# S5 phase tables: from GpSimd beside layer 0's first projections to VectorE beside layer 0's FFN

## The chip, the cores and the metric

One core of one Trainium2 chip runs the whole program. The metric is the device time of one execution in microseconds (us), and lower is better. The engines are called as the profile calls them: PE is TensorE's matmul, PEld its weight load, DVE is VectorE, ACT is ScalarE, POOL is GpSimd, and SP is SyncE, which here only issues DMAs (SPq is its queue).

## What is computed

The reference is a backbone block of two layers over 512 latent tokens and 256 context tokens of width 1024. Layer 0 mixes with SSD heads and RG-LRU blocks, layer 1 with HGRN2 heads and S5 groups, and a convolutional FFN of width 2816 stands behind each mixer. What the change touches is the S5 scan of layer 1, a complex diagonal recurrence with 16 groups of 64 states in each of two directions:

```
step = exp(log_step);  mag = exp(lam_re * step)
ar, ai = mag * cos(lam_im * step), mag * sin(lam_im * step)
h[t] = (ar + i ai) * h[t-1] + x[t]          (all 768 tokens, context first)
y = Re(h) c_re - Im(h) c_im
```

The kernel runs this recurrence over blocks of 8 tokens, 96 blocks in all. It turns the values of block n by the angle n times theta, where theta is 8 times lam_im times step, scans with the real factor mag to the power 8, and turns back. The cosines and sines of n times theta for n = 0 to 95, one row for each of 128 states (two directions of 64) and each of 16 groups, are the **phase tables** Ec and Es. They depend on parameters alone, not on the tokens.

## The kernel before

Everything is float32, and each big product is split into three matmuls of rounded halves (a high and a low part of both operands). The streams of the engines are put in order when the program is built: the build places instructions by their order in the source and by modelled times, so that neighbouring generators interleave on an engine, and each engine then runs its stream strictly in that order.

- **First projections of layer 0** (`xbc_phase`, L698). Twelve blocks of 128 channels, two to a weight panel of 256 columns. Each block takes 24 matmuls of 512 columns and 24 of 256, a four-tap convolution by ACT and DVE (L644) that reads the results from PSUM, SiLU, and a transpose. Beside them run the time-step path (`dt_phase`, L755), the modulation ticks and `s5_tables` (L827). The loop at L1200 calls one step of `s5_tables` for about 0.9 steps of `xbc_phase`.
- **`s5_tables`**. Step by step: lambda and step size are loaded, ar and ai are made, the reciprocal of the norm, then m8 (mag to the power 8) and, by three doublings of the angle (`twice`, L901), cosine and sine of theta. Then the phase tables (L919 to L933): starting from column 0 they are doubled seven times, from n columns to 2n, each time by one complex product (`cmul`, L892, six instructions: four multiplications, one subtraction, one addition). The constant ECV is 0, so all of them run on GpSimd over 16 groups at once; six more angle doublings run on DVE (18 instructions of 16 elements in a row). GpSimd's own DMA queue writes both tables to DRAM (`e_d`). The steps after that, on DVE, take powers of ar and ai (KP, eight copies at L952 to L955), load B and C, and multiply them (L974, `products` L988, `matrices` L1008).
- **Rest of layer 0's mixer**: the SSD steps, the RG-LRU, and the output projection. SSD is where GpSimd has its next work.
- **Layer 0's FFN** (`ffn`, L1383). Channel blocks f in groups of 8, 8 and 6. For each f there are gate and up projections, a 3 by 3 convolution on DVE, SiLU, and a product; for each group of f there are 8 output blocks m. Behind each f, each m of the first two groups, and the first four m of the last, `next(fill)` takes one step of a generator given from outside. At L1605 that generator is `l1_consts()` (one step) followed by 38 modulation ticks. A tick of `MT[3] = 5` makes five parts of the modulation vector: a 128 KB piece of `w_mod` comes by a DMA that SP issues, and DVE multiplies and adds it into `macc` (two instructions of 256 elements).
- **Layer 1**. The S5 scan (`quarter`, L1648) reads `e_d` back, four groups at a time (L1668), while layer 1's projections run.

The lines of the table before are these:

```
while n < 96:
    w = min(n, 96 - n)
    cmul(Ec[:, :, n:n + w], Es[:, :, n:n + w], Ec[:, :, 0:w], Es[:, :, 0:w],
         bc_mid(uc, w), bc_mid(us, w), et[:, :, :w], G if n > ECV else V)
    n *= 2
    if n < 96:
        uc, us = twice(f"v{n}", uc, us)
G.dma_start(e_d[0], Ec)
G.dma_start(e_d[1], Es)
```

Of the kernel before, what the change touches and what calls it, by code (L numbers as in the profile page):

```python
# [1 line left out]

# [1 line left out]

# [5 lines left out]
F32 = mybir.dt.float32  # L10
F32R = mybir.dt.float32r
AF = mybir.ActivationFunctionType
ALU = mybir.AluOpType
# [4 lines left out]
T = 768  # L18
# [10 lines left out]
MT = (1, 1, 4.5, 5, 1, 6, 1)  # L29
# [7 lines left out]
PSG = 0  # L37
# [11 lines left out]
ECV = 0  # L49
# [10 lines left out]
def bc_mid(ap, n):  # L60

    return ap.unsqueeze(2).broadcast_to([ap.shape[0], ap.shape[1], n])


def build(tc, I, out, dbg=None):
    nc = tc.nc
    V, S, G, PE, SP = nc.vector, nc.scalar, nc.gpsimd, nc.tensor, nc.sync
    if dbg is not None and "wrap" in dbg:
        V, S, G, PE, SP = [dbg["wrap"](e, n) for e, n in ((V, "V"), (S, "S"), (G, "G"), (PE, "PE"), (SP, "SP"))]
    es = ExitStack()  # L70
    cp = es.enter_context(tc.tile_pool(name="const", bufs=1, reuse_waits="tile"))
# [10 lines left out]
    def stt(o, a, s, b, op0, op1, eng=None):  # L82
        return (eng or V).scalar_tensor_tensor(o, a, s, b, op0=op0, op1=op1)  # L83


    def psx(name="px"):
        return pp.tile([128, 512], F32, tag="px", name=name, bufs=3)

    def psc(name="pc", n=256):
        return pp.tile([128, n], F32, tag="pc", name=name, bufs=2)  # L90
# [4 lines left out]
    def dump(name, ap):  # L95
        if dbg is not None and name in dbg:
            SP.dma_start(dbg[name], ap)
# [9 lines left out]
    def hcols(a, b):  # L107
        return [(HH[:, k, a:b], HL[:, k, a:b]) for k in range(8)]
# [129 lines left out]
    def mod_advance(q):  # L238

        q["stages"].pop(0)()  # L240
        if not q["stages"]:
            PEND.remove(q)
# [82 lines left out]
    def mod_tick():  # L325


        i = TICK[0]
        if i == NQ * LIM[0]:
            return  # L330
        l, j = MODSEQ[i // NQ]
        n = 1 if l == 1 and j >= 8 else 2
        if i % NQ == 0:
            MACC.append(macc())
        TICK[0] += 1
        mod_load()
        acc = MACC[-1]
        for k in range(8 // NQ):
            for e in range(n):
                prev = zero.broadcast_to([128, 256]) if i % NQ == 0 and k == 0 else acc[:, e]  # L340
                stt(acc[:, e], MST[i][:, k, :], sc[:, i % NQ * (8 // NQ) + k, e:e + 1], prev, ALU.mult, ALU.add)
        if i % NQ == NQ - 1:

            mod_pend(l, j, n, acc, LAG)
# [161 lines left out]
    def chain(*gs_):  # L506
        for g in gs_:
            yield from g
# [47 lines left out]
    for c, s_ in enumerate(src):  # L556
        t = ldp.tile([128, D], F32, tag=f"xin{c}", name=f"xin{c}")
# [55 lines left out]
    def mtick(r):  # L613
        for q in list(PEND):
            mod_advance(q)
        TA[0] += r
        while TA[0] >= 1.0:
            TA[0] -= 1.0
            mod_tick()
# [13 lines left out]
    h = hcols(0, T)  # L633
# [189 lines left out]
    kp_d = dr.tile([16, 16, 240], F32, name="kp_d")  # L823
    e_d = dr.tile([2, 128, 16, 96], F32, name="e_d")
    m8 = cp.tile([128, 16], F32, name="m8")

    def s5_tables():  # L827
        with tc.tile_pool(name="s5t", bufs=1, reuse_waits="tile") as tp:
            def t16(nm, shape=None):
                return tp.tile(shape or [128, 16], F32, name=nm, tag=nm)  # L830
# [58 lines left out]
            V.tensor_sub(zi, zi, ta)  # L889
            V.tensor_mul(zi, zi, den)  # L890

            def cmul(or_, oi, ar_, ai_, br, bi, t, eng):  # L892

                eng.tensor_mul(or_, ar_, br)
                eng.tensor_mul(t, ai_, bi)
                eng.tensor_sub(or_, or_, t)
                eng.tensor_mul(oi, ar_, bi)
                eng.tensor_mul(t, ai_, br)
                eng.tensor_add(oi, oi, t)

            def twice(nm, uc, us):  # L901

                c2, s2 = t16(f"{nm}c"), t16(f"{nm}s")
                stt(s2, uc, 2.0, us, ALU.mult, ALU.mult)
                stt(c2, us, -2.0, us, ALU.mult, ALU.mult)
                V.tensor_scalar(c2, c2, 1.0, None, op0=ALU.add)
                return c2, s2

            yield

            V.tensor_mul(m8, mag, mag)
# [1 line left out]
            V.tensor_mul(m8, m8, m8)  # L913
            uc, us = cs_, sn
            for i in range(3):
                uc, us = twice(f"u{i}", uc, us)
            yield

            with tc.tile_pool(name="s5e", bufs=1, reuse_waits="tile") as ep:  # L919
                Ec, Es = ep.tile([128, 16, 96], F32, name="Ec"), ep.tile([128, 16, 96], F32, name="Es")  # L920
                et = ep.tile([128, 16, 64], F32, name="et")
                V.memset(Ec[:, :, 0:1], 1.0)
                V.memset(Es[:, :, 0:1], 0.0)
                n = 1
                while n < 96:
                    w = min(n, 96 - n)
                    cmul(Ec[:, :, n:n + w], Es[:, :, n:n + w], Ec[:, :, 0:w], Es[:, :, 0:w],
                         bc_mid(uc, w), bc_mid(us, w), et[:, :, :w], G if n > ECV else V)
                    n *= 2
                    if n < 96:  # L930
                        uc, us = twice(f"v{n}", uc, us)
                G.dma_start(e_d[0], Ec)
                G.dma_start(e_d[1], Es)  # L933
            yield

            KP = [t16("kpr", [128, 9, 16]), t16("kpi", [128, 9, 16])]
            V.memset(KP[0][:, 0, :], 1.0)
# [4 lines left out]
            for k in (1, 2, 4):  # L942

                top = [KP[q][:, k:k + 1, :].broadcast_to([128, k, 16]) for q in range(2)]
                cmul(KP[0][:, k + 1:2 * k + 1, :], KP[1][:, k + 1:2 * k + 1, :], KP[0][:, 1:k + 1, :], KP[1][:, 1:k + 1, :],
                     top[0], top[1], kt[:, :k, :], V)
# [25 lines left out]
            bb = [t16("bbr", [128, 16, 16]), t16("bbi", [128, 16, 16])]  # L972
            tq = t16("tq", [128, 16, 16])
            cmul(bb[0], bb[1], B[0], B[1], bc_mid(zr, 16), bc_mid(zi, 16), tq, V)  # L974

            bs = [t16("bsr", [128, 16, 48]), t16("bsi", [128, 16, 48])]
# [220 lines left out]
    with tc.tile_pool(name="xbc", bufs=2, side="right", reuse_waits="tile") as xp:  # L1197
        s5t = s5_tables()
        acc = 0.0
        for i, _ in enumerate(xbc_phase(xp)):  # L1200
            acc += S5T
            while acc >= 1.0:
                acc -= 1.0
                next(s5t, None)
            if i == SSD0:
                for _ in s5t:
                    pass
                ssdp = sp_ctx.enter_context(tc.tile_pool(name="ssd", bufs=2, reuse_waits="tile"))
                ssd = ssd_phase(ssdp)
            if i >= SSD0 and (i - SSD0) % 2 == 0:  # L1210
                next(ssd)
# [290 lines left out]
    X = [xfp.tile([128, T], F32, name=f"xf{k}") for k in range(8)]  # L1502
# [14 lines left out]
    wfirst = [[], []]  # L1517
# [6 lines left out]
    norm = Norm(stats, X, T, lambda tag, n: ssdp.tile([128, n], F32, tag="xw" if tag == "diag" else "xt", name=tag, bufs=2), h, 0, "gffn", 3)  # L1524
    rest = norm.early()
# [19 lines left out]
    def lower_bound(pool):  # L1545
        l0, l1 = PS("lbl", 0, 6), PS("lbl", 6, 6)
        t = [pool.tile([128, 6], F32, name=f"lbt{i}") for i in range(7)]
        mx, e0, e1, s_, x_, a, b = t
        V.tensor_tensor(mx, l0, l1, op=ALU.max)
        for src, e in ((l0, e0), (l1, e1)):  # L1550
            V.tensor_sub(x_, src, mx)
            act(e, x_, AF.Exp)
            V.tensor_scalar(e, e, 1e-37, None, op0=ALU.max)
            act(a, e, AF.Ln)
            V.tensor_sub(a, x_, a)
            V.tensor_scalar(a, a, 1.0, 0.0, op0=ALU.add, op1=ALU.max)
            V.tensor_mul(e, e, a)
        V.tensor_add(s_, e0, e1)
        V.reciprocal(s_, s_)
        V.tensor_mul(e0, e0, s_)  # L1560
        V.tensor_mul(e1, e1, s_)
        V.tensor_add(e1, e0, e1)
        V.tensor_sub(lb, e1, e0)
        V.tensor_scalar(omlb, lb, -1.0, 1.0, op0=ALU.mult, op1=ALU.add)

    def l1_consts():
        with tc.tile_pool(name="l1c", bufs=1, reuse_waits="tile") as cp1:
            lower_bound(cp1)
        yield
# [17 lines left out]
    def nxt0(stats, pool):  # L1587
# [9 lines left out]
        def fin(pools):  # L1597
            for k in range(8):
                SP.dma_start(x2_d[k], X[k][:, XS])
                dump(f"x2_{k}", X[k])  # L1600
            FP.extend([norm, rest, pools])
        return rest, mid, fin

    FP = []
    ffn(0, X, T, norm, rest, wfirst, done0, h, nxt0, chain(l1_consts(), (mtick(MT[3]) for j in range(38 + 4 * PSG))))  # L1605
    norm, rest, pools = FP
    blk = [(psx(), psc()) for d in range(2)]

# [359 lines left out]
    X = []  # L1968
# [74 lines left out]
    h = hcols(0, 512)  # L2043
    norm = Norm(stats, X, 512, lambda tag, n: xqp.tile([128, n], F32, tag=tag, name=tag, bufs=2), h, 1, "gffn", 3)
    rest = norm.early()
# [67 lines left out]
```

## Time and profile before

| what | value |
|---|---|
| median of 3 runs | 2139.82 us (2135.62 to 2142.2) |
| the profiled execution | 2138.01 us, its span in the trace 2136.3 us |
| PE, PEld | 2022.4 us (95%), 1699.5 us (80%) |
| DVE | 1571.1 us (74%) |
| ACT | 872.8 us (41%) |
| POOL | 273.0 us (13%) |
| mean granted TensorE clock | 0.975 |

The span runs from the first to the last instruction of the trace, and 1.7 us of the profiled execution lie around it. Busy shares are means over stages with different limits, so the stage in which a piece of work lies has to be looked at by itself. In a timeline each line is one instruction or a run of equal ones: start, duration, engine, source line, operation, output and inputs, and in brackets the idle time before it with what ended that idle time. Two DVE instructions can overlap a little at their ends, so the distance from one start to the next is what an instruction costs in a busy stream, and its duration is slightly more.

### The profile page before, as it was taken

How to read it: one execution, taken by the hardware profiler on the slowest of the kernel's cores; microseconds unless marked ns; L12 is line 12 of the kernel's file. 1: busy time of each engine (PE TensorE's matmuls, PEld its weight loads, DVE VectorE, ACT ScalarE, POOL GpSimd, SP SyncE). 2: the span in 40 equal slices, each digit the busy share in tenths (PEclk: the TensorE clock that was granted, in tenths of full speed). 3: DMA queues.
4: the chain of work that ended last, by engine and by line, in shares of the span. 5: the costliest groups of instructions: out<-in, count | busy, mean ns of one | idle time of the engine just before them, and what ended most of it. 6: DMA issues, size and time to landing. Idle time of an engine off the chain costs nothing.

```text
span 2136.3 us, 32686 instructions
## 1 busy us (share of the span) xinstructions
PE 2022.4 (95%) x12738; PEld 1699.5 (80%) x12738; DVE 1571.1 (74%) x2916; ACT 872.8 (41%) x1276; POOL 273.0 (13%) x234
## 2 busy tenths in 40 slices
PE   8969989898898999999999999999999899999998
PEld 4848778787677888888888888897877688888887
DVE  5898898767778888868765656656876678667484
ACT  4625577586533442212321323324444344223234
POOL 2142333344421000000000000110011100000000
PEclk9979899999999999999999999999999999999999
DMA  9437535435676322333234112554421123222321
GB/s 332 132 102 206 152 98 168 123 97 165 225 242 215 99 87 94 112 121 116 94 118 139 62 50 94 152 160 147 126 71 58 40 80 99 97 82 98 99 84 55
DMA packets 283019, 261.09 MB, mean 122 GB/s; under 512 B 23406, under 2 KB 263061, under 8 KB 282865
## 3 DMA queue, kind: packets, MB, share of 16 engines
q1 hardware_dynamic: 257504, 243.35, 35.8%
q10 hardware_dynamic: 24464, 13.75, 2.3%
q8 instruction: 100, 1.64, 0.3%
q0 software_dynamic: 896, 1.90, 0.2%
q14 instruction: 55, 0.44, 0.1%
HBM read 224.17 MB, written 34.78 MB: 121 GB/s over the span
## 4 chain that ended last, share of the span: by engine, by line
PE 62%; DVE 6%; DMA 4%; POOL 1%; issue 1%; ACT 1%; SPq 0%; POOLq 0%; DVEq 0%; ACTq 0%
PE px L215 34%; PE pc L215 10%; PE pu L215 6%; PE pseg L215 4%; DMA mst<-in_w_mod_dram 1%; DVE macc L83 1%; PE pmodt L352 1%; PE pv L222 1%; PE pv L223 1%; PE pv L224 1%; POOL kc L1816 1%; PE plv L1858 1%; PE pob L215 1%; DMA xt<-xtok_d 0%; PE py L1711 0%
## 5 line engine op out<-in xcount | busy, mean ns | idle before, releaser
L80 ACT ACTIVATE whi<-st 128x1024 fp32r<-128x1024 f32 (+1 forms) x197 | 203.4, 1037 | 565.3 <-PE pc L215 365.1
L215 PE MATMUL px<-HH,whi 128*128 128x512 f32 (+2 forms) x1016 | 407.8, 403 | 15.3 <-DVE xbct L83 7.9
L215 PE MATMUL px<-HH,wlo 128*128 128x512 f32 (+2 forms) x1016 | 404.4, 398 | 0.0
L215 PE MATMUL px<-HL,whi 128*128 128x512 f32 (+2 forms) x1016 | 403.4, 397 | 0.9 <-DVE HL L83 0.9
L193 DVE TENSOR_TENSOR wlo<-st,whi 128x1024 fp32r<-128x1024 f32 (+1 forms) x197 | 237.5, 1209 | 78.3 <-ACT whi L80 76.3
L83 DVE SCALAR_TENSOR_TENSOR macc<-mst,sc,macc 128x256 f32<-128x256 f32 x434 | 216.9, 530 | 65.9 <-DMA mst<-in_w_mod_dram 64.8
L83 DVE SCALAR_TENSOR_TENSOR fa<-px,par,fa 128x441 f32<-128x441 f32 (+2 forms) x352 | 241.8, 691 | 8.2 <-ACT fa L80 2.2
L215 PEld LDWEIGHTS px<-HH,whi 128*128 128x128 f32 (+1 forms) x1016 | 192.0, 189 | 59.5 <-issue 9.6
L215 PEld LDWEIGHTS px<-HL,whi 128*128 128x128 f32 (+1 forms) x1016 | 191.8, 189 | 44.5 <-DVE HL L83 1.9
L215 PEld LDWEIGHTS px<-HH,wlo 128*128 128x128 f32 (+1 forms) x1016 | 191.8, 189 | 43.7
L215 PE MATMUL pc<-HH,whi 128*128 128x256 f32 x728 | 207.2, 286 | 4.6 <-ACT ge L80 3.2
L215 PE MATMUL pc<-HH,wlo 128*128 128x256 f32 x728 | 206.9, 285 | 0.0
L215 PE MATMUL pc<-HL,whi 128*128 128x256 f32 x728 | 206.9, 285 | 0.0
L215 PEld LDWEIGHTS pc<-HH,whi 128*128 128x128 f32 x728 | 137.8, 190 | 8.0 <-ACT ge L80 4.0
L80 ACT ACT_TABLE_LOAD x104 | 133.4, 1283 | 19.2 <-issue 5.4
L215 PEld LDWEIGHTS pc<-HL,whi 128*128 128x128 f32 x728 | 138.2, 190 | 1.1
L215 PEld LDWEIGHTS pc<-HH,wlo 128*128 128x128 f32 x728 | 138.2, 190 | 0.5
L215 PE MATMUL px<-fhi,wlo 128*128 128x512 f32 x304 | 120.4, 396 | 0.0
L215 PE MATMUL px<-fhi,whi 128*128 128x512 f32 x304 | 120.3, 396 | 0.0
L215 PE MATMUL px<-flo,whi 128*128 128x512 f32 x304 | 119.8, 394 | 0.0
L1815 POOL TENSOR_TENSOR kc<-kc,e 128x255 f32<-128x255 f32 x6 | 7.1, 1181 | 853.0 <-ACT kc L80 675.6
L215 PE MATMUL pu<-HH,wlo 128*128 128x512 f32 (+1 forms) x192 | 74.3, 387 | 0.0
(645 smaller groups left out, 4291.1 us busy)
## 6 DMA issues: line engine op xcount, KB each, us to landing
mst<-in_w_mod_dram SPq DMA_DIRECT2D x312, 128.0 KB, 2.2
st<-in_ffn_w_gate_dram SPq DMA_DIRECT2D x22, 1024.0 KB, 5.0
st<-in_ffn_w_up_dram SPq DMA_DIRECT2D x22, 1024.0 KB, 5.0
st<-in_ev_w_in_dram SPq DMA_DIRECT2D x18, 1024.0 KB, 6.4
st<-in_ffn_w_down_dram SPq DMA_DIRECT2D x16, 1024.0 KB, 5.0
bc<-cum_d SPq DMA_DIRECT2D x24, 512.0 KB, 6.2
sth<-in_od_w_in_dram SPq DMA_DIRECT2D x24, 512.0 KB, 4.0
st<-in_w_mod_dram SPq DMA_DIRECT2D x9, 1024.0 KB, 11.6
```

Of the source, the lines that this page charges most:

```text
L80: return S.activation(o, i, f, bias=bias, scale=scale, **kw)
L83: return (eng or V).scalar_tensor_tensor(o, a, s, b, op0=op0, op1=op1)
L193: (eng or V).tensor_sub(lo, src, hi.bitcast(F32))
L215: PE.matmul(o, ww[:, k, :M], hh[k][part][:, sl], start=(first and q == 0 and a == 0), stop=(stop and q == last and a == 2))
L222: PE.matmul(o, hh[k][0][:, sl], whi[:, k % 4, :], start=(k == 0), stop=False)
L223: PE.matmul(o, hh[k][0][:, sl], wlo[:, k % 4, :], start=False, stop=False)
L224: PE.matmul(o, hh[k][1][:, sl], whi[:, k % 4, :], start=False, stop=(k == 7))
L352: PE.matmul(pt[:, 2 * h_ + e:2 * h_ + e + 1], acc[:, e, h_ * 128:(h_ + 1) * 128], ones[:, 0:1], start=True, stop=True)
L1815: G.tensor_mul(kc[:, 0, 0:255], kc[:, 0, 0:255], e0[:, 0:255])
L1816: G.tensor_mul(kc[:, 1, 1:256], kc[:, 1, 1:256], e1[:, 1:256])
L1858: PE.matmul(v3[r:r + 32, c, :], kk(j), qq(j), start=True, stop=True, tile_position=(0, r))
```

## The change

The functions `cmul` and `twice` move out of `s5_tables`. `s5_tables` now only keeps cosine and sine of theta in a small constant tile `u8`, and has one step fewer. A new generator `s5_phases` makes the six doubled angles, and then builds the tables for four groups at a time on DVE, with the same doublings, in four steps for each four groups; SP issues the two writes to `e_d` for each. A new helper `both_of` advances two generators together. The FFN of layer 0 now gets `l1_consts()` followed by `s5_phases()` on one side and the 38 modulation ticks on the other, one step of each for each `next(fill)`.

```diff
@@ -1,4 +1,5 @@
 from contextlib import ExitStack
+from itertools import zip_longest
 
 import numpy as np
 
@@ -823,6 +824,48 @@
     kp_d = dr.tile([16, 16, 240], F32, name="kp_d")
     e_d = dr.tile([2, 128, 16, 96], F32, name="e_d")
     m8 = cp.tile([128, 16], F32, name="m8")
+    u8 = cp.tile([128, 2, 16], F32, name="u8")
+
+    def cmul(or_, oi, ar_, ai_, br, bi, t, eng):
+
+        eng.tensor_mul(or_, ar_, br)
+        eng.tensor_mul(t, ai_, bi)
+        eng.tensor_sub(or_, or_, t)
+        eng.tensor_mul(oi, ar_, bi)
+        eng.tensor_mul(t, ai_, br)
+        eng.tensor_add(oi, oi, t)
+
+    def twice(pool, nm, uc, us):
+
+        c2, s2 = [pool.tile([128, 16], F32, name=nm + x, tag=nm + x) for x in "cs"]
+        stt(s2, uc, 2.0, us, ALU.mult, ALU.mult)
+        stt(c2, us, -2.0, us, ALU.mult, ALU.mult)
+        V.tensor_scalar(c2, c2, 1.0, None, op0=ALU.add)
+        return c2, s2
+
+    def s5_phases():
+
+        with tc.tile_pool(name="s5e", bufs=1, reuse_waits="tile") as ep:
+            lad = [(u8[:, 0], u8[:, 1])]
+            for i in range(6):
+                lad.append(twice(ep, f"v{i}", *lad[-1]))
+            yield
+            for g in range(0, 16, 4):
+                gs_ = slice(g, g + 4)
+                Ec, Es = [ep.tile([128, 4, 96], F32, name=x, tag=x) for x in ("Ec", "Es")]
+                et = ep.tile([128, 4, 64], F32, name="et", tag="et")
+                V.memset(Ec[:, :, 0:1], 1.0)
+                V.memset(Es[:, :, 0:1], 0.0)
+                for i, (uc, us) in enumerate(lad):
+                    n = 1 << i
+                    w = min(n, 96 - n)
+                    cmul(Ec[:, :, n:n + w], Es[:, :, n:n + w], Ec[:, :, 0:w], Es[:, :, 0:w],
+                         bc_mid(uc[:, gs_], w), bc_mid(us[:, gs_], w), et[:, :, :w], V)
+                    if i in (3, 4, 5):
+                        yield
+                SP.dma_start(e_d[0, :, gs_], Ec)
+                SP.dma_start(e_d[1, :, gs_], Es)
+                yield
 
     def s5_tables():
         with tc.tile_pool(name="s5t", bufs=1, reuse_waits="tile") as tp:
@@ -889,23 +932,6 @@
             V.tensor_sub(zi, zi, ta)
             V.tensor_mul(zi, zi, den)
 
-            def cmul(or_, oi, ar_, ai_, br, bi, t, eng):
-
-                eng.tensor_mul(or_, ar_, br)
-                eng.tensor_mul(t, ai_, bi)
-                eng.tensor_sub(or_, or_, t)
-                eng.tensor_mul(oi, ar_, bi)
-                eng.tensor_mul(t, ai_, br)
-                eng.tensor_add(oi, oi, t)
-
-            def twice(nm, uc, us):
-
-                c2, s2 = t16(f"{nm}c"), t16(f"{nm}s")
-                stt(s2, uc, 2.0, us, ALU.mult, ALU.mult)
-                stt(c2, us, -2.0, us, ALU.mult, ALU.mult)
-                V.tensor_scalar(c2, c2, 1.0, None, op0=ALU.add)
-                return c2, s2
-
             yield
 
             V.tensor_mul(m8, mag, mag)
@@ -913,25 +939,10 @@
             V.tensor_mul(m8, m8, m8)
             uc, us = cs_, sn
             for i in range(3):
-                uc, us = twice(f"u{i}", uc, us)
-            yield
-
-            with tc.tile_pool(name="s5e", bufs=1, reuse_waits="tile") as ep:
-                Ec, Es = ep.tile([128, 16, 96], F32, name="Ec"), ep.tile([128, 16, 96], F32, name="Es")
-                et = ep.tile([128, 16, 64], F32, name="et")
-                V.memset(Ec[:, :, 0:1], 1.0)
-                V.memset(Es[:, :, 0:1], 0.0)
-                n = 1
-                while n < 96:
-                    w = min(n, 96 - n)
-                    cmul(Ec[:, :, n:n + w], Es[:, :, n:n + w], Ec[:, :, 0:w], Es[:, :, 0:w],
-                         bc_mid(uc, w), bc_mid(us, w), et[:, :, :w], G if n > ECV else V)
-                    n *= 2
-                    if n < 96:
-                        uc, us = twice(f"v{n}", uc, us)
-                G.dma_start(e_d[0], Ec)
-                G.dma_start(e_d[1], Es)
-            yield
+                uc, us = twice(tp, f"u{i}", uc, us)
+            yield
+            for q, t_ in enumerate((uc, us)):
+                V.tensor_copy(u8[:, q], t_)
 
             KP = [t16("kpr", [128, 9, 16]), t16("kpi", [128, 9, 16])]
             V.memset(KP[0][:, 0, :], 1.0)
@@ -1601,8 +1612,13 @@
             FP.extend([norm, rest, pools])
         return rest, mid, fin
 
+    def both_of(*gs_):
+
+        for _ in zip_longest(*gs_):
+            yield
+
     FP = []
-    ffn(0, X, T, norm, rest, wfirst, done0, h, nxt0, chain(l1_consts(), (mtick(MT[3]) for j in range(38 + 4 * PSG))))
+    ffn(0, X, T, norm, rest, wfirst, done0, h, nxt0, both_of(chain(l1_consts(), s5_phases()), (mtick(MT[3]) for j in range(38 + 4 * PSG))))
     norm, rest, pools = FP
     blk = [(psx(), psc()) for d in range(2)]
 
```

## Rows read from the trace of the kernel before

**Rows 1.** windows of four stretches: length, then busy PE, PEld, DVE, ACT, POOL, PEclk, DMA, GB/s

```profile
98.00:129.20 31.20, 19.67 (x100) 16.10 (x98) 30.96 (x86) 13.43 (x19) 26.39 (x44) 0.87 0.16 55
129.20:150.00 20.80, 11.65 (x75) 7.51 (x76) 20.80 (x36) 1.93 (x3) 0.09 (x1) 0.66 0.42 117
150.00:200.00 50.00, 50.00 (x329) 42.69 (x330) 44.36 (x74) 20.44 (x34) 4.99 (x5) 0.98 0.68 195
785.00:900.00 115.00, 115.00 (x674) 100.96 (x673) 94.86 (x175) 32.63 (x40) 0.00 (x0) 1.00 0.34 110
```

**Rows 2.** PE's timeline, 110 to 155 us: the three longest waits

```profile
119.58 0.45 PE L970 MATMUL ps5c<-ident,cst 128*128 128x128 f32 x1 [5.62 <-DVE xbct L83]
...
132.18 0.76 PE L215 MATMUL px<-HH,whi 128*128 128x512 f32 x1 [7.88 <-DVE xbct L83]
...
147.12 0.42 PE L1018 MATMUL pkp<-n,bsr 128*48 128x128 f32 x2 [3.06 <-DVE kp L1023]
```

**Rows 3.** POOL's timeline, 80 to 420 us: first and last of the tables, and the next

```profile
98.09 0.29 POOL L895 TENSOR_TENSOR et<-Es,u2s 128x16 f32<-128x16 f32 x1 [35.30 <-DVE u2c L83]
...
128.71 0.58 POOL L933 DMA_DIRECT2D e_d<-Es  x1 [0.30 <-POOL Es L899]
194.68 1.09 POOL L1109 TENSOR_SCALAR_AFFINE_SELECT bc<-bc 128x1024 f32<-128x1024 f32 x1 [65.40 <-DMA bc<-cum_d]
```

**Rows 4.** DVE's timeline, 80 to 205 us: instructions beside POOL's, and alone

```profile
108.87 0.72 DVE L952 COPY pwr<-kpr 64x144 f32<-64x144 f32 x1
...
110.67 0.60 DVE L954 COPY pqr<-kpr 64x128 f32<-64x128 f32 x1
...
115.66 1.10 DVE L803 TENSOR_TENSOR wend<-wend,dtv 128x192 f32<-128x192 f32 x1
116.68 0.74 DVE L83 SCALAR_TENSOR_TENSOR xbct<-px,par,xbct 128x511 f32<-128x511 f32 x1
...
121.33 1.30 DVE L895 TENSOR_TENSOR tq<-bi,zi 128x256 f32<-128x256 f32 x1
...
126.33 0.41 DVE L898 TENSOR_TENSOR tq<-bi,zr 128x256 f32<-128x256 f32 x1
126.67 0.28 DVE L979 COPY bsr<-bbr 64x256 f32<-64x256 f32 x1
...
127.31 1.25 DVE L980 COPY bsr<-bbr 64x256 f32<-64x256 f32 x1
...
128.87 0.29 DVE L980 COPY bsi<-bbi 64x256 f32<-64x256 f32 x1
129.19 0.75 DVE L83 SCALAR_TENSOR_TENSOR xbct<-px,par,xbct 128x511 f32<-128x511 f32 x1
```

**Rows 5.** the same timeline: small instructions and the starts of the next

```profile
105.32 0.16 DVE L83 SCALAR_TENSOR_TENSOR v64c<-v32s 128x16 f32<-128x16 f32 x1
105.41 0.32 DVE L894 TENSOR_TENSOR kpr<-kpr 128x32 f32<-128x32 f32 x1
...
107.71 0.21 DVE L895 TENSOR_TENSOR kt<-kpi 128x64 f32<-128x64 f32 x1
107.85 0.21 DVE L897 TENSOR_TENSOR kpi<-kpr,kpi 128x64 f32<-128x64 f32 x1
```

**Rows 6.** windows of 2 us: columns as in the first group

```profile
150.00:152.00 2.00, 2.00 (x11) 1.49 (x12) 2.00 (x3) 0.00 (x0) 0.00 (x0) 0.50 0.22 49
```

**Rows 7.** waits, us in total, times, longest: ACT, SP 785 to 1010, PE 760 to 1350

```profile
ACT whi L80 <- PE pc L215: 140.5, 24, 8.2
...
SPq L322 <- DVE macc L83: 147.9, 76, 33.6
...
PE px L215 <- ACT HH L80: 1.0, 1, 1.0
```

**Rows 8.** the page's DMA issues: KB each, us to landing

```profile
mst<-in_w_mod_dram SPq DMA_DIRECT2D x312, 128.0 KB, 2.2
```

**Rows 9.** instructions on tile e_d: count, ns, first and last start

```profile
L1668 SPq DMA_DIRECT2D E<-e_d x8: 320/383/507, 1337.5 to 1420.7; - x8
```

## Prediction

> **What bounds the kernel now.** I read the windows by stage first, because a mean over the span mixes stages with different limits. Between 98 and 150 us PE is busy for 31 of 52 us and DVE for all but 0.2 us [rows 1]. From 150 to 200 us PE has no gap [rows 1]. So in the stage that loses its table work DVE is the bound, and PE pays for it. PE's own timeline says the same: its three longest waits there end with DVE, 5.62, 7.88 and 3.06 us, 16.6 us together [rows 2]. [...] In layer 0's FFN it is the other way round: from 785 to 900 us PE is busy for 115.00 of 115 us and DVE idle for 20.1 us [rows 1]. Work taken from DVE in the first stage is worth its full length; work given to DVE in the second costs nothing while it fits into the idle time.
>
> GpSimd itself is not waited for: its tables run from 98 to 129 us, and its next instruction starts at 194.68 us, after a wait for a DMA [rows 3]. What counts is what the tables do to DVE while they run. The copy of 64x256 at L980 takes 1.25 us beside them and 0.29 us right behind them; a product of 128x256 takes 1.30 us beside them, and 0.41 us five us later [rows 4]. The convolution, which reads PSUM, takes 0.74 us beside them and 0.75 us after [rows 4].
>
> **The change, part by part.**
> *Slowed instructions (removed).* I count in distances between starts, since DVE is never idle there. From L952 at 108.87 to L803 at 115.66 us are eight copies and one small addition, 6.8 us [rows 4]; without 0.5 us for the addition 6.3 us. Alone, a copy of more elements costs 0.3 us [rows 4], so eight cost 2.4 and 3.9 us go. These copies also transpose, and no row shows one undisturbed: their own price lies between 0.3 and 0.6, the shortest of the eight [rows 4], which leaves a saving of 1.5 us at worst. I take 0.3, as the pair at L980 is the same kind of copy. L803 costs 1.02 and would cost at most the 0.34 of a wider product [rows 4]: 0.7. From 121.33 to 129.19 us six products and four copies take 7.9 us; at 0.34 and 0.3 they take 3.2 [rows 4]: 4.6. The small products around 105 to 110 us are slowed too: 0.32 us for 32 elements, where 64 elements cost 0.21 later [rows 5]. Six of them at an estimated 0.2 each make 1.2. Sum 10.4 us, at worst 8.0.
> *Six doublings (removed here).* 18 instructions at 0.09 [rows 5] make 1.6 us. Two memsets go and two copies into u8 come: even.
> *GpSimd's 42 products and its two table writes.* Nobody waits for them [rows 3], so beyond the slowing they are worth nothing here.
> DVE thus gets through this stage 12.0 us earlier (9.6 at worst). All three waits of PE end with DVE and the stage after 150 us is PE without a gap, so PE's end of the stage moves by as much. A shorter idle time may also spare PE some of the half speed after it: between 0 and 1 us (the window at 0.50 [rows 6]); I take 0. What follows depends on these streams alone and moves rigidly.
>
> *The tables on DVE (added).* For four groups the products are 4, 8, 16, 32, 64, 128 and 128 elements wide, six instructions each. Distances: 0.09 for 16 elements, 0.14 for 64 [rows 5], 0.34 for 256 [rows 4]; between them I estimate 0.11 for 32 and 0.21 for 128. That is 18 x 0.09 + 6 x 0.11 + 6 x 0.14 + 12 x 0.21 = 5.6, with two memsets 5.8, four times 23; with the ladder of 18 small ones 25 us. By the order of the fill steps the ladder, the first four groups and most of the second fall beside f = 0 to 7, hence 785 to 900 us: 94 instructions, 1.6 + 5.8 + 3.3 = 10.7 us against 20.1 idle [rows 1]. The cover is DVE's idle time; if it were gone, each us would reach PE through a PSUM buffer read late. Cost on the path 0, at most 2 us, as no row shows this mixture.
> An instruction of 64 elements is recorded with 0.21 us, and the next starts 0.14 us after it [rows 5]. [...]
>
> *Waits added.* SP now issues eight writes of 192 KB, and each holds SP until DVE has finished a four-group table; behind it stand the pieces of w_mod and the FFN's weight panels. SP already waits there for DVE's macc, 76 times and 147.9 us, while PE waited 1.0 us in the longest entry of the whole stage [rows 7]. Weights are ahead: ACT waits 140.5 us for PE to free the buffers of the split weights [rows 7]. Late next is one piece of w_mod per group. A piece of 128 KB lands in 2.2 us [rows 8], so four times 2.2 = 9 us of DVE idling, in idle time. The memset that opens the next group waits until the last tables have been written; behind it on DVE stand macc and the next convolution, and PE behind that. Two writes are at most 2 x 3.3 us by size, and the next group comes a fill step later: 0. GpSimd's queue loses the two writes, which nobody missed. The reader starts at 1337.5 us [rows 9], long after.
> *The ticks* come one fill step earlier, 38 as before: 0. *One step fewer in s5_tables* moves KP and the products a step forward against the convolutions: the work is the same, its order is not; between -3 and +3 us, 0 taken.
>
> Sum: 2138.0 - 12.0 = **2126.0 us**, from the profiled execution (span 2136.3 and 1.7 around it), which lies 1.8 us under the median of the runs. Its own range: 2122 to 2131.
>
> **Rivals.**
> *The waits go altogether.* If the new order gives PE enough to do, it regains 16.6 us of waits and the half speed behind them; from the means, 20 us busy at 0.87 and 12 at 0.66 [rows 1], 6.5 us more: 2115. Against it: DVE stays full after 129 us, when GpSimd is done [rows 1]. Chance 0.10.
> *The gain is taken back.* A step forward can put one four-group product, a dozen instructions at about 0.65 us (the 511-wide convolution's 0.75 less the overlap [rows 4]), ahead of a convolution that PE waits for: 7.8 us lost, 2134. Or the slow instructions are slow by themselves and only the 1.6 us go: 2136; the pair at L980 speaks against that. Together 0.19.
> *Slower: SP held in the FFN.* One mechanism: a table write stands in SP's queue ahead of a weight panel, DVE comes to the tables late because macc waits for its pieces, and PE runs out of weights. A stall like the 5.62 us one [rows 2] with some 2 us lost at half speed after it costs 8 us; one for each of the four writes 32, and 2138 + 32 - 12 = 2158. It decides from 3 us per group on. For it: SP waits for DVE most of the time there; against it: ACT's 140.5 us of waiting for PE [rows 7]. 0.11. [...]
>
> **How the numbers follow.** Forecast 0.60, rivals 0.10, 0.19, 0.11. A measurement of this kernel can tell 0.3%, or 6.4 us, from no change: faster means under 2133.4. The forecast and the first rival lie there (0.70), the second within (0.19), the last above (0.11). The range takes in the forecast, the bounds of its terms and both milder rivals, and leaves out the slow one: 2112 to 2138.
>
> **What would show it.** Right: between 98 and 150 us POOL idle, the copies at L952 near 0.3 us, L980 the same for both halves, PE's waits there several us shorter, PE without gaps from about 138 us, and layer 0's FFN as long as before with DVE busy for some 10 us more in its first 115 us. Wrong: copies still at 0.6 to 1.0 without GpSimd; new waits of PE for products at L988 to L1023; PE waiting in the FFN for split weights or for a convolution; or a shift at 150 us that is gone by 560 us.

## The result, and the profile after

The changed kernel takes 2161.55 us (2159.83 to 2165.15), the kernel before beside it 2141.01 us: ratio 1.0098, 95% interval [1.0074, 1.0121]. It is slower, against a forecast of 2126.0 us, and lies outside the range of 2112 to 2138. Lines are numbered by each kernel's own listing; in the changed kernel L215 has become L216, L83 L84, L193 L194, and L952 L963.

The page of the changed kernel: its span, PE with busy time and share, then PE's busy tenths and granted clock in 40 slices.

```profile
span 2158.1 us, 32856 instructions
PE 2039.2 (94%) x12738; PEld 1709.7 (79%) x12738; DVE 1591.1 (74%) x3092; ACT 884.0 (41%) x1283; POOL 248.1 (11%) x190
...
PE   8889988998798999999999999999999899999998
...
PEclk9989998999799999999999999999999999999999
```

PE is busy for 16.8 us longer and idle for 5.0 us longer than before, and the one slice at clock 7, the eleventh, lies at 540 to 593 us. That is neither the stage that lost the tables nor the one that got them. The same four windows as in [rows 1]:

```profile
98.00:129.20 31.20, 21.90 (x109) 18.14 (x110) 30.55 (x84) 10.08 (x14) 0.00 (x0) 0.78 0.26 72
129.20:150.00 20.80, 17.84 (x137) 13.32 (x136) 20.80 (x36) 6.21 (x11) 0.00 (x0) 0.84 0.50 139
150.00:200.00 50.00, 49.99 (x312) 42.85 (x310) 41.22 (x63) 27.65 (x40) 15.12 (x10) 1.00 0.72 215
785.00:900.00 115.00, 111.57 (x646) 97.83 (x646) 107.25 (x259) 36.85 (x46) 0.00 (x0) 0.99 0.33 107
```

From 98 to 150 us PE is busy for 39.7 us where it was 31.3 [rows 1]: the gain is there. (The fourth window is the same by the clock, but the FFN begins 15 us later in the changed kernel.) DVE's timeline shows the copy at L963, the product and the copy at L991 unslowed, against 0.72, 1.30 and 1.25 in [rows 4]:

```profile
102.64 0.42 DVE L832 TENSOR_TENSOR tq<-bi,zi 128x256 f32<-128x256 f32 x1
...
104.96 0.27 DVE L963 COPY pwr<-kpr 64x144 f32<-64x144 f32 x1
...
108.00 0.29 DVE L991 COPY bsr<-bbr 64x256 f32<-64x256 f32 x1
```

To see where it is lost I cut each trace at the same instructions. **A** runs from the first to the tenth of the twelve SiLUs of the convolution (ACT, `xbct<-xbct`), **B** from there to the first `xo<-px` on DVE (output projection of the RG-LRU), **C** to the first `fa<-fa,pu` (FFN), **D** to the 36th instruction that writes `xf`, **E** from the 61st of those to the last FFN product of layer 1. Lengths in us, from one profiled execution each. The ratio is that of a comparison's runs with runs of the kernel before beside them, an estimate with an interval; the quotient of the two medians can differ from it by about 0.001.

| kernel | ratio | A | B | C | D | E |
|---|---|---|---|---|---|---|
| before | 1 | 127.6 | 380.7 | 199.8 | 333.3 | 777.5 |
| changed | 1.0098 | 120.1 | 402.8 | 201.1 | 336.7 | 780.6 |
| e1_step_back | 0.9971 | 116.6 | 381.6 | 201.0 | 336.7 | 777.8 |
| e2_step_less | 1.0115 | 135.0 | 400.7 | 200.3 | 333.5 | 775.6 |
| e3_ffn_tables_added | 1.0023 | 128.9 | 385.6 | 201.2 | 337.0 | 776.3 |
| e4_gpsimd_writes_only | 0.9965 | 119.3 | 384.2 | 199.8 | 333.3 | 778.5 |
| e5_rate_up | 1.0019 | 119.4 | 385.3 | 205.4 | 337.4 | 781.9 |
| e6_tables_later | 0.9947 | 113.9 | 388.4 | 198.4 | 335.2 | 782.5 |
| e7_tables_not_computed | 1.0073 | 119.0 | 399.9 | 201.7 | 338.4 | 782.3 |
| e8_later_and_rate | 0.9971 | 115.8 | 380.4 | 200.6 | 336.7 | 783.2 |
| e9_ticks_early | 1.0021 | 129.2 | 382.8 | 200.5 | 337.0 | 781.2 |
| e10_step_back_ticks_late | 0.9942 | 114.6 | 382.4 | 198.5 | 334.1 | 780.3 |

The changed kernel gains 7.5 us in A, loses 22.1 in B, where the edit touches no instruction, and 3.4 in D. E goes with the set of runs and not with the kernel: 776 to 779 in the profiles of e1 to e4, 780 to 783 in the later ones, while the median of the kernel before rose from 2139.14 to 2142.89 and 2141.41. The changed kernel's 3 us there may be of that sort, and I build nothing on them.

Two of the prediction's signs of being wrong are there. At the start of B the changed kernel is 8 us ahead of the kernel before (193.9 against 202.2 us) and at its end 14 us behind (596.7 against 582.9), so the shift is lost within B. And PE waits in the FFN for a split weight; the part on what the FFN pays for takes this up.

Stage B as one window, and its last 96.7 us, first of the kernel before, then of the changed one (columns as in [rows 1]):

```profile
202.20:582.90 380.70, 339.17 (x1988) 289.51 (x1986) 308.09 (x383) 257.02 (x342) 158.39 (x93) 0.93 0.47 148
...
486.20:582.90 96.70, 80.19 (x455) 63.54 (x453) 72.13 (x80) 63.97 (x86) 48.03 (x30) 0.91 0.58 194
```
```profile
193.90:596.70 402.80, 352.28 (x1997) 298.60 (x1996) 312.06 (x372) 265.57 (x347) 156.49 (x92) 0.89 0.43 136
...
500.00:596.70 96.70, 74.96 (x379) 56.45 (x378) 70.26 (x74) 59.69 (x75) 55.42 (x34) 0.82 0.52 174
```

About the same matmuls, 9.0 us more of PE idling (50.5 against 41.5), and 13.1 us more of busy time at a clock of 0.89 instead of 0.93. What differs is their order. The SSD part makes twelve forward steps, each opened by two `pcbm` matmuls. Here is the seventh on PE's timeline, before and after:

```profile
369.44 0.47 PE L1100 MATMUL pcbm<-cch,bch 128*128 128x128 f32 x2
```
```profile
417.67 0.47 PE L1111 MATMUL pcbm<-cch,bch 128*128 128x128 f32 x2
```

It is 48 us late, although B began 8 us earlier. Counted in projection matmuls (`px`, `pc`, `pz`) that PE has run by then, the twelve steps stand at 576, 601, 624, 744, 897, 1014, 1281, 1398, 1665, 1778, 2001, 2007 before, and at 576, 590, 624, 777, 894, 1161, 1545, 1662, 1929, 1992, 2007, 2160 after. Of the last seven, six come 147 to 264 matmuls later, so fewer projections are left to cover the SSD steps at the end. The second line of the two windows above shows that end, the last 96.7 us of B: PE is busy for 74.96 us at a clock of 0.82, before for 80.19 at 0.91, and 244 projection matmuls start in it, before 344.

### The profile page after: what moved, and what is told of

Its sections match the earlier page's. It is cut to its first block, busy times and chain, and to the rows that moved or that the text cites. A ratio compares the mean times of both kernels' runs of the same rounds, so it can differ in the third digit from the quotient of the medians.

```text
span 2158.1 us, 32856 instructions
## 1 busy us (share of the span) xinstructions
PE 2039.2 (94%) x12738; PEld 1709.7 (79%) x12738; DVE 1591.1 (74%) x3092; ACT 884.0 (41%) x1283; POOL 248.1 (11%) x190
## 4 chain that ended last, share of the span: by engine, by line
PE 72%; DVE 15%; DMA 6%; ACT 3%; issue 2%; POOL 2%; SPq 0%; ACTq 0%; POOLq 0%; DVEq 0%
PE px L216 36%; PE pc L216 12%; PE pu L216 6%; PE pseg L216 4%; DMA mst<-in_w_mod_dram 2%; DVE macc L84 2%; PE pmod L299 1%; DVE wlo L194 1%; DVE bc L1118 1%; ACT L81 1%; DVE xbct L84 1%; PE pz L224 1%; PE pmodt L353 1%; DMA bc<-cum_d 1%; PE pz L225 1%
## 5 line engine op out<-in xcount | busy, mean ns | idle before, releaser
L216 PE MATMUL px<-HH,wlo 128*128 128x512 f32 (+2 forms) x1016 | 404.0, 398 | 9.5 <-DVE wlo L194 9.5
L216 PE MATMUL px<-HH,whi 128*128 128x512 f32 (+2 forms) x1016 | 407.0, 402 | 4.5 <-DVE xbct L84 2.3
L216 PE MATMUL px<-HL,whi 128*128 128x512 f32 (+2 forms) x1016 | 403.7, 398 | 0.8 <-DVE HL L84 0.8
L194 DVE TENSOR_TENSOR wlo<-st,whi 128x1024 fp32r<-128x1024 f32 (+1 forms) x197 | 238.8, 1216 | 105.6 <-ACT whi L81 103.4
L84 DVE SCALAR_TENSOR_TENSOR macc<-mst,sc,macc 128x256 f32<-128x256 f32 x434 | 215.4, 530 | 56.6 <-DMA mst<-in_w_mod_dram 55.2
L84 DVE SCALAR_TENSOR_TENSOR fa<-px,par,fa 128x441 f32<-128x441 f32 (+2 forms) x352 | 241.7, 692 | 7.2 <-ACT fa L81 1.2
L216 PEld LDWEIGHTS px<-HH,wlo 128*128 128x128 f32 (+1 forms) x1016 | 192.2, 189 | 53.8 <-DVE wlo L194 10.2
L216 PEld LDWEIGHTS px<-HH,whi 128*128 128x128 f32 (+1 forms) x1016 | 192.4, 190 | 48.8 <-issue 3.4
L216 PEld LDWEIGHTS px<-HL,whi 128*128 128x128 f32 (+1 forms) x1016 | 192.0, 189 | 44.6 <-DVE HL L84 1.9
L216 PE MATMUL pc<-HH,whi 128*128 128x256 f32 x728 | 206.4, 285 | 8.4 <-DVE u L84 4.5
L216 PE MATMUL pc<-HL,whi 128*128 128x256 f32 x728 | 206.4, 284 | 0.0
L216 PE MATMUL pc<-HH,wlo 128*128 128x256 f32 x728 | 206.2, 284 | 0.0
L216 PEld LDWEIGHTS pc<-HH,whi 128*128 128x128 f32 x728 | 137.8, 190 | 11.6 <-issue 5.3
L216 PEld LDWEIGHTS pc<-HL,whi 128*128 128x128 f32 x728 | 138.1, 190 | 1.5 <-issue 0.2
L216 PEld LDWEIGHTS pc<-HH,wlo 128*128 128x128 f32 x728 | 138.1, 190 | 0.7
L216 PE MATMUL px<-fhi,whi 128*128 128x512 f32 x304 | 120.5, 396 | 0.0
L216 PE MATMUL px<-flo,whi 128*128 128x512 f32 x304 | 120.5, 396 | 0.0
L216 PE MATMUL px<-fhi,wlo 128*128 128x512 f32 x304 | 119.5, 393 | 0.0
L216 PE MATMUL pu<-HL,whi 128*128 128x512 f32 (+1 forms) x192 | 74.7, 389 | 0.0
```

The costliest lines, as they stand in the source:

```text
L194: (eng or V).tensor_sub(lo, src, hi.bitcast(F32))
L216: PE.matmul(o, ww[:, k, :M], hh[k][part][:, sl], start=(first and q == 0 and a == 0), stop=(stop and q == last and a == 2))
```

## The experiments

My theory after this reading: the missing step of `s5_tables` lets the build place everything behind it otherwise, and that order costs the 20 us. The rival was that the table work on DVE, or SP's writes, do it.

### One step put back, and one taken from the kernel before

The changed kernel with an empty step behind the `u8` copies, no instruction more or less:

```diff
             for q, t_ in enumerate((uc, us)):
                 V.tensor_copy(u8[:, q], t_)
+            yield
```

> The changed kernel with one empty step put back into the S5 table generator, behind the copies into u8. Theory 'order' (the missing step moves every later step of the generator half a block forward, the build then places the SSD steps later among the RG-LRU projections, and these late steps stand without cover at the end of that stage): the loss of some 22 us between 200 and 600 us goes, what is left is the gain before 200 us (8 us) less the loss in layer 0's FFN (4 to 5 us) and in layer 1 (3 us at most): 2134 to 2142 us, ratio 0.997 to 1.000. Theory 'FFN' (the tables on DVE in layer 0's FFN are what costs): as the changed kernel, ratio 1.008 to 1.011.

Measured: 2134.76 us, ratio 0.9971 [0.9954, 0.9987]. The twelve SSD steps stand exactly where they stood before, B is 381.6 us, A is 11.0 us shorter than before. So the missing step had cost 3.5 us in A too (120.1 against 116.6). PE's longest wait of the changed kernel there, for the low half of a split weight (`wlo`), is not among the waits of the kernel with the step:

```profile
PE px L216 <- DVE wlo L194: 7.0, 1, 7.0
```

The counterpart, the kernel before with the step behind its table writes taken out, all work where it was:

```diff
                 G.dma_start(e_d[1], Es)
-            yield
```

> The kernel before, with nothing changed but one step less in the S5 table generator: the step after the table writes is joined to the one behind it; the tables stay on GpSimd. Theory 'order': the same late SSD steps as in the changed kernel and a loss of 14 to 24 us, ratio 1.007 to 1.011, without any table work in the FFN. Theory 'FFN': no change, ratio 0.998 to 1.002.

Measured: 2165.66 us, ratio 1.0115 [1.0088, 1.0142], a little above the forecast. Its SSD steps have the changed kernel's places, and B is 400.7 us. A gets longer too: PE's waits from 98 to 160 us have one of 18.5 us, longer than any of [rows 2].

```profile
PE px L215 <- DVE wlo L193: 18.5, 1, 18.5
```

One `yield` with no work in it is worth 1.3% between the changed kernel and the first (1.0098 / 0.9971) and 1.15% between the second and the kernel before. There is no run with an empty step at the end of the generator instead; as built, it gives PE, DVE, ACT and POOL the same instructions in the same order as the changed kernel. So the order depends on the step's place, not on the number of steps.

### The rest of the change by itself

The kernel before with the four-group tables on DVE added in the FFN, and GpSimd's tables left where they were:

```diff
+    e2_d = dr.tile([2, 128, 16, 96], F32, name="e2_d")
...
+            lad = [(m8, m8)]
...
-    ffn(0, X, T, norm, rest, wfirst, done0, h, nxt0, chain(l1_consts(), (mtick(MT[3]) for j in range(38 + 4 * PSG))))
+    ffn(0, X, T, norm, rest, wfirst, done0, h, nxt0, both_of(chain(l1_consts(), s5_phases()), (mtick(MT[3]) for j in range(38 + 4 * PSG))))
```

> The kernel before, untouched in its first stages, with the changed kernel's table generator added to layer 0's FFN on DVE (its results go to a tensor that nobody reads, its angles are dummies). The marks of the two traces differ by 4 to 5 us more behind the first eight channel blocks of that FFN than ahead of them. Theory 'order': plus 4 to 5 us, ratio 1.001 to 1.003. Theory 'FFN': plus 20 us, ratio 1.009.

Measured: 2144.63 us, ratio 1.0023 [1.0007, 1.0039]; D is 337.0 us, the changed kernel's 336.7. The FFN loses 3.7 us of its own. This kernel has both the tables and the pairing by `both_of`; the part on what the FFN pays for takes them apart.

The kernel before with GpSimd's products replaced:

```diff
             def cmul(or_, oi, ar_, ai_, br, bi, t, eng):
+                if eng is G:
+                    for o_ in (or_, t, or_, oi, t, oi):
+                        G.memset(o_, 0.5)
+                    return
```

> The kernel before, with GpSimd's 42 products of the tables replaced by memsets of the same tiles (the tables are left out of the computation); no instruction of PE, DVE or ACT changes its place. [...] The forecast's first term: DVE 10.4 us earlier at 129 us and the run 8 to 12 us faster, ratio 0.994 to 0.997. Rival (the copies and products are slow by themselves): no change, ratio 0.999 to 1.001. Between them if the gain is partly taken back behind 200 us.

This kernel leaves the tables' values out. Measured: 2133.37 us, ratio 0.9965 [0.9947, 0.9983]; A is 8.3 us shorter, with the six doublings still in it. A copy that took 0.72 us at L952 [rows 4] takes 0.27:

```profile
110.92 0.27 DVE L956 COPY pwr<-kpr 64x144 f32<-64x144 f32 x1
```

The memsets did not run beside these copies: they wait for no angle and were done at 70.9 us. So the run shows the eight copies at 0.26 to 0.30 us with GpSimd idle, against 0.60 to 1.06 beside its products in the kernel before, and leaves open whether its reads or its writes slow them. What it showed of the memsets themselves stands in the last section.

### Another way to move the SSD steps

The changed kernel with the planned price of an SSD element on DVE altered:

```diff
-SSDR = 0.15
+SSDR = 0.25
```

> The changed kernel with one number altered: the planned price of an SSD element on VectorE, SSDR, from 0.15 to 0.25, and no step put back. By its planned order this gives the SSD steps places near those of the kernel before (the 7th of the twelve at 984 projection matmuls, where before has 1014, the changed kernel 1161 and the step put back 1014). Order theory: what the changed kernel loses lies in the places of the SSD steps, so the stretch from the last silu of the convolution to the first output projection of the RG-LRU takes 381 to 386 us and not 403, and the time is near that of the step put back, 2133 to 2143 (0.996 to 1.002). Rival, that the missing step itself or the DVE-built tables make the stretch long whatever the order: 402 us again, 2157 to 2165 (1.008 to 1.012).

(The mark that these texts call the last SiLU is the tenth, as defined above.) Measured: 2148.6 us, ratio 1.0019 [1.0001, 1.0038]; B is 385.3 us. The step is still missing, DVE still builds the tables, and 17.5 of the 22.1 us are back: it is the places that count. (On PE the last seven stand at 984, 1281, 1368, 1370, 1665, 1778 and 2001.) The ratio is at the edge of the forecast and the time above it; C is 205.4 us in this order, 4 us longer than with the step put back. An order that suits one stage is not free in the next.

How much B varies without a change of places can be read from the table: in the eight kernels whose twelve SSD steps stand where they stood before, B is 380.4 to 388.4 us; in the three with the changed kernel's places it is 399.9 to 402.8.

### What the FFN pays for

Three kernels asked for the 3.5 us of D. With the step put back, the tables were moved eight and fourteen fill steps later (the label of the second speaks of a rate; none is altered):

```diff
+            yield
...
-both_of(chain(l1_consts(), s5_phases()), (mtick(MT[3]) ...
+both_of(chain(l1_consts(), iter([None] * 8), s5_phases()), (mtick(MT[3]) ...
```

> The changed kernel with the step put back and eight empty steps ahead of the phase tables, so that their first group begins later in the FFN. Theory: the 3.5 us that the FFN loses with the tables come from the first blocks, where matmuls waited for VectorE behind table instructions; later there is room, so the FFN's stretch falls from 337 to 333 to 334 us and the whole from 2134.8 to about 2131 (0.994 to 0.997). Rival, that VectorE's added 25 us cost PE something wherever they stand in this FFN: 336 to 337 us, 2133 to 2136 (0.996 to 0.999).

> The changed kernel with the step put back and fourteen empty steps ahead of the phase tables. The same question as with eight, one point further: if the cost falls with the distance from the FFN's first blocks, the FFN's stretch is 333 to 334 us and the time no more than with eight, about 2131 (0.994 to 0.997); if the tables now meet the layer-1 constants or the end of the FFN, 335 to 337 us, or the stretch behind the FFN grows by 1 to 3 us.

Measured: ratios 0.9947 [0.9932, 0.9963] and 0.9971 [0.9956, 0.9986], D 335.2 and 336.7 us. The second point doesn't continue the first, so distance is not what decides; the theory that the table instructions stand in the way was in trouble. The next run ended it. In the changed kernel the ladder and the products were taken out, so that it leaves the tables' values out:

```diff
-            for i in range(6):
-                lad.append(twice(ep, f"v{i}", *lad[-1]))
...
-                for i, (uc, us) in enumerate(lad):
...
+                V.memset(Ec, 1.0)
+                V.memset(Es, 0.0)
+                for i in range(3):
+                    yield
```

> The changed kernel with its 168 table instructions and six doublings left out: the tables are filled by memsets and written to memory as before, so the S5 phases are not computed. The SSD steps keep the changed kernel's places. Order theory: the SSD and RG-LRU stretch stays at 401 to 404 us, the FFN goes from 336.7 to 333 to 334, the whole is 2155 to 2159 (1.007 to 1.009). Rival, that the table work in the FFN is what made the changed kernel slower than before: 2126 to 2142 (0.994 to 1.001).

Measured: 2159.98 us, ratio 1.0073 [1.0054, 1.0092], as the order theory has it; but D is 338.4 us, where 333 to 334 were expected, with no table computed in it. PE's waits in D, of this kernel:

```profile
PE px L216 <- DVE wlo L194: 2.9, 1, 2.9
```

The kernel before has none there, the changed one one of 2.5 us. DVE's timeline ahead of that weight part, first in the kernel before, then in the changed one:

```profile
788.29 0.42 DVE L1432 TENSOR_TENSOR fa<-fa,pc 128x256 f32<-128x256 f32 x1 [2.04 <-PE pc L215]
788.63 0.88 DVE L83 SCALAR_TENSOR_TENSOR macc<-mst,sc,zero 128x256 f32<-128x256 f32 x2
789.42 1.22 DVE L193 TENSOR_TENSOR wlo<-st,whi 128x1024 fp32r<-128x1024 f32 x1
```
```profile
802.10 0.42 DVE L1443 TENSOR_TENSOR fa<-fa,pc 128x256 f32<-128x256 f32 x1 [1.29 <-PE pc L216]
802.44 1.27 DVE L84 SCALAR_TENSOR_TENSOR macc<-mst,sc,macc 128x256 f32<-128x256 f32 x3
803.81 0.96 DVE L1447 TENSOR_TENSOR flo<-fa,fhi 128x768 fp32r<-128x768 f32 x1
804.68 1.22 DVE L194 TENSOR_TENSOR wlo<-st,whi 128x1024 fp32r<-128x1024 f32 x1
```

No table instruction stands ahead of the late `wlo`; three parts of the modulation (`macc`) and a `flo`, the low half of split activations, do. They are the ticks, which `both_of` starts one fill step earlier. So the kernel before, with that alone:

```diff
-chain(l1_consts(), (mtick(MT[3]) for j in range(38 + 4 * PSG)))
+both_of(l1_consts(), (mtick(MT[3]) for j in range(38 + 4 * PSG)))
```

> The kernel before with one thing of the change alone: the ticks of the modulation run beside l1_consts in the FFN's fill chain instead of behind it, so that the five ticks of each step come one step earlier. The phase tables stay on GpSimd, and the SSD steps keep their places. Theory, since the FFN also took 338 us where no table was computed in it: the FFN's loss is the ticks' doing, whose multiply-adds (0.48 us each) now stand ahead of a weight part that PE waits for in the first blocks; the stretch from the first FFN multiplication to the last xf takes 336 to 337 us instead of 333.3, and the time is 1.000 to 1.003 of before, about 2142 in the scale of the last comparison plus 2 to 4. Rival, that the table work or the table writes are needed for the loss: 333 to 334 us, 0.998 to 1.000.

Measured: 2144.13 us, ratio 1.0021 [1.0007, 1.0036]; D 337.0 us. The same order on DVE, the same wait of PE, and a granted clock of 0.92 in the 10 us after it, where the kernel before has 1.00 (the last fence, this kernel first):

```profile
790.85 1.27 DVE L84 SCALAR_TENSOR_TENSOR macc<-mst,sc,macc 128x256 f32<-128x256 f32 x3
792.07 0.96 DVE L1437 TENSOR_TENSOR flo<-fa,fhi 128x768 fp32r<-128x768 f32 x1
792.94 1.22 DVE L194 TENSOR_TENSOR wlo<-st,whi 128x1024 fp32r<-128x1024 f32 x1
```
```profile
PE px L216 <- DVE wlo L194: 2.5, 1, 2.5
```
```profile
797.00:807.00 10.00, 10.00 (x53) 8.62 (x53) 6.98 (x14) 2.18 (x3) 0.00 (x0) 0.92 0.78 248
...
792.00:802.00 10.00, 10.00 (x59) 8.66 (x57) 9.29 (x18) 2.29 (x3) 0.00 (x0) 1.00 0.71 235
```

### The change without its two side effects

The changed kernel with the step put back and the ticks one step later again; all the table work stays on DVE in the FFN:

```diff
+            yield
...
-both_of(chain(l1_consts(), s5_phases()), (mtick(MT[3]) ...
+both_of(chain(l1_consts(), s5_phases()), chain([None], (mtick(MT[3]) ...
```

> The changed kernel with the step put back (as in the first experiment) and the ticks moved back to where they stood, one step later, with the tables beside them. Theory: the FFN's stretch falls from 336.7 to 333 to 334 us although VectorE still does all the table work there, and the whole lies 2 to 4 us under the step put back alone: 0.9945 to 0.996 of before. Rival, that 25 us of table work on VectorE cost the FFN something by themselves: 336 to 337 us and 0.996 to 0.998.

Measured: 2129.05 us (2121.95 to 2138.0), ratio 0.9942 [0.9923, 0.9961], just under the forecast and the lowest of all. The intervals of e1, e4, e6 and e8 overlap its own, so the FFN's gain is shown by the stage and not by the time. D is 334.1 us: the table work, 28 us from start to start on DVE, of which 23.5 lie in D, cost it 0.8. (The rest lies in C, which is no longer than before.) PE's wait and what stands ahead of it:

```profile
PE px L216 <- DVE wlo L194: 1.0, 1, 1.0
```
```profile
774.63 0.87 DVE L84 SCALAR_TENSOR_TENSOR macc<-mst,sc,zero 128x256 f32<-128x256 f32 x2
775.42 1.22 DVE L194 TENSOR_TENSOR wlo<-st,whi 128x1024 fp32r<-128x1024 f32 x1
```

Two parts of the modulation again, as before the change. The third part and the `flo` in front of `wlo` make 1.3 us of DVE's time, and PE's wait was longer by 1.5. Over all twelve kernels D is 333.3 to 334.1 us in the four with the ticks in their old place and 335.2 to 338.4 in the eight with early ticks, whether DVE computes tables there or not.

## Why the prediction was wrong, step by step

- **Slowed instructions and doublings, 12.0 us earlier (9.6 at worst): right.** With the step put back A is 11.0 us shorter (11.0 to 13.7 in the four kernels that have it). The slowed instructions alone, forecast at 10.4 with 8.0 as the lower bound, measured 8.3 in the memset run. The copy whose undisturbed price no row showed takes 0.27 us; I had taken 0.3.
- **"What follows depends on these streams alone and moves rigidly": the step that failed.** The streams themselves were not the same. With it fell "*One step fewer in s5_tables* ... the work is the same, its order is not; between -3 and +3 us, 0 taken". I looked for the order's effect among the convolutions, near the edit; there the step cost 3.5 us, at the edge of my bound (A is 119.0 to 120.1 us in the changed kernel, e5 and e7 without it, 113.9 to 116.6 in the four with it). (The loop takes 0.9 steps of `s5_tables` for each step of `xbc_phase`; the front part says it the other way round.) Further on, where I took the streams to be rigid, it measured 20.0 us in B alone when the one `yield` was taken out of the kernel before, and 21.2 between the changed kernel (402.8) and the same with the step back (381.6). The front part had said how the build orders streams, by source order and modelled times; I priced a disturbance of that planner by the work it moved, which was nothing.
- **"*The ticks* come one fill step earlier, 38 as before: 0": failed too, with a smaller size.** 3.7 us in D (e9): one wait of 2.5 us behind three `macc` and a `flo`, and 1.2 us more of busy time (334.5 us against 333.3), with a granted clock of 0.92 from 797 to 807 us, where the kernel before has 1.00. I had counted the ticks and not what they stand ahead of.
- **Tables on DVE, cost 0, at most 2: right.** 0.8 us, for 28 us of work instead of the 25 estimated. DVE's instructions of 128 elements are recorded with 0.28 us and start 0.20 apart, against my 0.21 (783.15, 783.35, 783.55 in e10).
- **Waits added, 0: nothing against it.** SP's writes stand in e10 and cost no more than 0.8 us with all the rest.
- **The slow rival had the sign and the wrong mechanism.** It wanted SP held by table writes. In e9 there are no such writes, and D is as long as in the changed kernel. That its 2158 us lie so near the measured time is chance.

With both orders restored, the sum of the priced steps is what the chip gives: 0.9942 of the profiled 2138.0 is 2125.6 us (2121.5 to 2129.7 by the interval), the forecast 2126.0. That it agrees to less than a microsecond is luck: the interval is 4 us to either side, and B varies by 8 us in kernels with the same places.

Left open: why the planner answers a step with this order. The runs show that it does, and what the order costs, not which modelled time tips it. Nor do they split B's loss between single waits.

## What to carry to other kernels

Where a build orders the streams by itself, an edit has two prices: its work, and the new order of everything planned behind it. Compare the two orders first, by counting a few landmark instructions along one engine's stream; if they differ far from the edit, hold the order with an empty step and measure the work alone. A helper that pairs two generators also shifts one of them: look which instruction now stands ahead of a weight or a PSUM read that PE waits for.

## What the runs showed of the hardware that I had not expected

In the memset run, GpSimd's memsets run from 61.7 to 70.9 us. Two kinds of DVE instructions with two inputs in SBUF are as fast beside them as in the kernel before (two `macc` 0.88 us, there 0.87; two `wlo` of 256 elements 1.55 us, there 1.55 with GpSimd idle). A `tensor_scalar`, one input in SBUF, and the small copies just behind it, whose input `ps` lies in PSUM, are not done before the last memset is over. GpSimd's timeline, then DVE's, in that run:

```profile
70.36 0.54 POOL L896 MEMSET Es<- 128x512 f32 x1
```
```profile
67.15 0.88 DVE L83 SCALAR_TENSOR_TENSOR macc<-mst,sc,macc 128x256 f32<-128x256 f32 x2 [0.18 <-DMA mst<-in_w_mod_dram]
...
68.00 2.93 DVE L835 TENSOR_SCALAR step<-step 128x16 f32<-128x16 f32 x1
...
68.06 2.86 DVE L847 COPY lr<-ps 128x16 f32<-128x16 f32 x1
```

and the same two in the kernel before:

```profile
67.67 0.15 DVE L835 TENSOR_SCALAR step<-step 128x16 f32<-128x16 f32 x1
...
67.74 0.17 DVE L847 COPY lr<-ps 128x16 f32<-128x16 f32 x1
```

All end at 70.9 us, with the memset at 70.36. Beside memsets `macc` keeps its length; beside GpSimd's products a DVE product took 1.30 us instead of 0.41 [rows 4]. The `tensor_scalar` is not done with the memset that is in progress at 68.00 us: it ends with the last of the six that start behind that one, 0.47 us apart, and is recorded with 2.9 us where it has 0.15 in the kernel before. Why it takes longer there and `macc` does not, no row shows. Nor do the rows tell whether the memsets held the two copies or the `tensor_scalar` in front of them did.
